# Order of the value products in the second mixer: upper and lower attention weights of a key block side by side

## The chip, the core and the metric

The kernel runs on one core of one Trainium2 chip. The metric is device time in microseconds, from the start of the program to its end. An execution with the profiler gives the trace from which every row below is taken; its own time and its span stand beside the median of the unprofiled runs.

## The reference: what is computed

A two-layer streaming encoder trunk for 1024 prompt frames and 8 x 16 sample frames (1152 columns in all), width 1024, in float32. Layer 0 has a first mixer (stick-breaking attention beside a convolution), layer 1 a second mixer (chunk-band attention with a learned relative bias); each layer ends with a squared-ReLU MLP of width 4096. The change is in the second mixer, whose attention is

```
s = einsum('bqhd,bkhd->bhqk', q, k) * HEAD_DIM**-0.5 + rel_bias[:, rel]
p = softmax(where(mask, s, -inf))          # own chunk of 64 and the 8 chunks before it
o = einsum('bhqk,bkhd->bqhd', p, v)
```

with 16 heads of 64. For the prompt a block of 128 queries sees at most five blocks of 128 keys.

## The kernel before

Activations lie transposed (features on partitions, tokens on columns). A float32 matrix product is made of float32r products: each operand is split into an upper part and a lower rest (`split`: ScalarE copies the upper part, L185, VectorE subtracts it for the rest, L186). A projection takes three products for one (upper-upper, upper-lower, lower-upper: `SPLIT`), so its first two follow each other on the same stationary weights.

The second mixer (`mixer1`) goes through 8 pairs of heads, p = 0 to 7. A pair has eight jobs, i = 0, 1 (the head) times t = 0 to 3 (256 queries). A job has two score steps (`one`: TensorE products of queries with upper keys, L1201, and lower keys, L1202, both on the same stationary queries; the softmax with maximum L1165 on VectorE, exponential L1168 on ScalarE, reciprocal L1169 and scaling L1170 on VectorE), and then its weighing steps, `split_weigh_steps`. These gather the key blocks of the job into groups of at most 512 columns: (256, 128) for t = 0, (256, 256) and (256, 128) for t = 1, (256, 256), (256, 256) and (128, 128) for t = 2 and 3; 144 groups in all. `turn` transposes a group's weights on TensorE (L455, tile `tp`, shown as tpc) and splits them into `wh` and `wl` (shown as whc and wlc). `prod` multiplies them with the values (L467, into the accumulator av, shown as avc): the stationary operand is a key block's values, upper and lower halves side by side, which occupy 128 columns; the moving operand is 256 or 128 columns of wh or wl. `finish` adds the two halves of av (L475 on ScalarE, L477 on VectorE) and stores the result in cat_d.

Between these steps stand the projections of the next pair (L225 into psc, 128x384), the sample streams' attention, and `expand` (L348 to L353: upper and lower keys and scaled queries of the next pair, each a 64x1024 operation on ScalarE or VectorE, with copies by DMA from GpSimd). For p = 7 there is no next pair; there `ready_chunks` loads finished pieces (cr) back from cat_d and splits them into cat, and `part_out` begins the output projection (L225 into psoa) on them.

The steps are merged into one program order by a table of costs (`merge`), and a scheduler of the language then sets each engine's final order from its own model of times: an instruction that its model holds back lets others on its engine pass. So a change of the order in one step can move instructions elsewhere. Each engine works through its own queue in order; ScalarE, VectorE, GpSimd and SyncE (which issues most loads) have one each.

Of the kernel before, what the change touches and what calls it, by code (L numbers as in the profile page):

```python
# [124 lines left out]
def tile_trunk(ctx, tc, ins, outs):  # L125
# [17 lines left out]
    def bank(name):  # L143
        return psum.tile([P, 512], F32, tag="ps", name=name)
# [38 lines left out]
    def split(hi, lo, src):  # L183

        ACT(hi, src, AF.Copy)  # L185
        return tt(lo, src, f(hi), ALU.subtract)  # L186
# [247 lines left out]
    def split_weigh_steps(vs, wk, cat, i, t, blocks, name, scored):  # L434


        order = sorted(blocks.keys, key=lambda j: -len(blocks.keys[j]))
        groups, cur, used = [], [], 0
        for j in order:
            n = P * len(blocks.keys[j])  # L440
            if used + n > 512:
                groups.append((cur, used))
                cur, used = [], 0
            cur.append((j, used, n))
            used += n
        groups.append((cur, used))
        nmm = 2 * len(order)
        st = {"done": 0, "w": {}}

        def turn(gi):  # L450
            items, used = groups[gi]
            tp = bank(f"tp{name}{gi}")
            for j, c0, n in items:
                for q, tile_q in enumerate(blocks.keys[j]):
                    nc.tensor.transpose(tp[:, c0 + q * P:c0 + (q + 1) * P], blocks.get(j, tile_q), ident)  # L455
            wh = wk.tile([P, 512], F32R, tag="wt", name=f"wh{name}{gi}")
            wl = wk.tile([P, 512], F32R, tag="wt", name=f"wl{name}{gi}")
            split(wh[:, :used], wl[:, :used], tp[:, :used])
            st["w"][gi] = (wh, wl)

        def prod(gi):
            if gi == 0:
                st["av"] = bank(f"av{name}")
            for src in st["w"][gi]:
                for j, c0, n in groups[gi][0]:
                    o0 = 0 if 2 * t in blocks.keys[j] else P
                    mm(st["av"][:, o0:o0 + n], vs[:, j, i].rearrange("p a d -> p (a d)"), src[:, c0:c0 + n],  # L467
                       start=st["done"] == 0, stop=st["done"] == nmm - 1)
                    st["done"] += 1

        def finish():
            own = slice(64 * i, 64 * i + 64)
            av = st["av"]
            tmp = wk.tile([P, 256], F32, tag="av", name=f"at{name}")
            ACT(tmp[own], av[64:128, :256], AF.Copy)  # L475
            piece = wk.tile([P, 256], F32, tag="cat", name=f"cp{name}")
            tt(piece[own], av[0:64, :256], tmp[own], ALU.add)  # L477
            cat.put(piece, own, t * 256, 256)

        def pcost(gi):  # L480
            return sum(2 * max(n, 256) * PASS for _, _, n in groups[gi][0])

        def tcost(gi):
            return groups[gi][1] / P * 109

        last = len(groups) - 1
        def dcost(gi):
            return 60 + groups[gi][1] / 0.96

        def turns(gi):  # L490
            return Step(tcost(gi), lambda: turn(gi), dcost(gi), f"turn{name}{gi}", None if gi else scored, 4500)

        lag = 4500 if cat.layer == 0 else 2500

        def prods(gi):
            if gi < last:
                return Step(pcost(gi), lambda: prod(gi), 0.0, None, f"turn{name}{gi}", lag)
            return Step(pcost(gi), lambda: (prod(gi), finish()), 330.0, f"out{name}", f"turn{name}{gi}", lag)

        steps = [turns(0)]  # L500
        for gi in range(1, last + 1):
            steps += [turns(gi), prods(gi - 1)]
        steps.append(prods(last))
        return steps
# [1441 lines left out]
```

## Time and profile before

| | us |
|---|---|
| median of 3 runs | 2752.49 (2751.73 to 2756.9) |
| the profiled execution, its own time | 2748.28 |
| its span, first to last instruction | 2746.5 |
| TensorE products (PE) busy | 2666.7, 97% |
| VectorE (DVE) / ScalarE (ACT) / GpSimd (POOL) busy | 2090.2 / 1388.1 / 328.2 |

The span is 1.8 us shorter than the execution's own time, which in turn is 4.2 us below the median of the unprofiled runs; differences worked out in the trace are added to the median. PE counts the products, PEld the loads of stationary weights that run beside them. In a row of a timeline the columns are start, duration, engine, line, operation, written tiles <- read tiles, shapes, and the count where equal instructions follow each other; in brackets the idle time of the engine before the first and what ended it. Ends of products are modelled, so consecutive products overlap in the rows: the distance between starts tells the pace.

### The profile page before, as it was taken

What the parts mean: (1) busy time and instruction counts of PE and PEld (TensorE: products, weight loads), DVE (VectorE), ACT (ScalarE), POOL (GpSimd) and SP (SyncE); (2) the same over time, 40 slices, a digit from 0 to 9 for tenths busy, and PEclk for the clock granted to TensorE, in tenths of its full rate; (3) what the DMA queues carried; (4) which work ended last, traced back from release to release, by engine and by line L of the source; (5) the groups of instructions that cost most, each with busy time, mean ns of one, the idle gap of its engine ahead of it and who ended that gap; (6) DMA issues with size and microseconds to landing.
All of it is one profiled execution on the core that took longest, in us unless ns stands there. A gap on an engine that the chain in (4) does not pass through costs nothing.

```text
span 2746.5 us, 50585 instructions
## 1 busy us (share of the span) xinstructions
PE 2666.7 (97%) x19362; PEld 2553.7 (93%) x19362; DVE 2090.2 (76%) x4117; ACT 1388.1 (51%) x2906; POOL 328.2 (12%) x599
## 2 busy tenths in 40 slices
PE   8999898999999999999999999998999999999998
PEld 8987776799999999999999999997999999999998
DVE  8999998888777755768577777778787777647577
ACT  5344457755444543435355555556555545434344
POOL 1000101041111100000011111110221111100001
PEclk9999999999999999999999999999999999999999
DMA  4434446454344377435444444446534334674344
GB/s 158 124 113 141 122 137 228 144 176 140 142 143 145 133 271 248 118 102 174 141 138 144 133 139 139 132 134 231 180 127 144 143 140 144 232 259 134 96 125 145
DMA packets 173203, 422.90 MB, mean 154 GB/s; under 512 B 25968, under 2 KB 53808, under 8 KB 170912
## 3 DMA queue, kind: packets, MB, share of 16 engines
q1 hardware_dynamic: 135696, 288.38, 33.4%
q0 software_dynamic: 37120, 131.27, 13.9%
q8 instruction: 152, 2.49, 0.4%
q14 instruction: 91, 0.75, 0.1%
q10 hardware_dynamic: 144, 0.02, 0.0%
HBM read 289.60 MB, written 117.34 MB: 148 GB/s over the span
## 4 chain that ended last, share of the span: by engine, by line
PE 71%; DVE 4%; ACT 2%; DMA 1%; issue 1%; DVEq 0%; SPq 0%; ACTq 0%; POOLq 0%
PE pd L1690 26%; PE um L1461 25%; PE psc L225 10%; PE avc L467 2%; PE tpc L455 2%; PE zc L1201 1%; PE zc L1202 1%; PE psoa L225 1%; PE so L602 1%; PE zs L568 1%; DVE xr L1367 0%; PE psob L225 0%; DMA cr<-cat_d 0%; ACT s L1168 0%; ACT whc L185 0%
## 5 line engine op out<-in xcount | busy, mean ns | idle before, releaser
L225 PE MATMUL psc<-h,hl_wc 128*128 128x384 f32 x1728 | 327.2, 340 | 0.0
L225 PEld LDWEIGHTS psc<-h,hl_wc 128*128 128x128 f32 x1728 | 296.9, 188 | 13.3 <-issue 10.9
L1461 PE MATMUL um<-sl,hl_m 128*128 128x288 f32 x1548 | 240.8, 296 | 0.0
L1461 PEld LDWEIGHTS um<-sl,hl_m 128*128 128x128 f32 x1548 | 218.2, 189 | 0.0
L1690 PE MATMUL pd<-tm,hl_wd 128*128 128x288 f32 x1584 | 214.7, 295 | 0.0
L1690 PEld LDWEIGHTS pd<-tm,hl_wd 128*128 128x128 f32 x1584 | 211.3, 189 | 0.0
L735 DVE SCALAR_TENSOR_TENSOR y<-u,dw,y 128x1024 f32<-128x1024 f32 (+1 forms) x232 | 178.1, 810 | 0.6
L225 PE MATMUL psp<-h,hl_wi 128*128 128x384 f32 x864 | 165.7, 344 | 0.0
L1468 ACT ACTIVATE hdm<-hdm 128x288 f32<-128x288 f32 x192 | 84.7, 442 | 156.5 <-DVE hdm L1467 154.8
L225 PEld LDWEIGHTS psp<-h,hl_wi 128*128 128x128 f32 x864 | 150.8, 191 | 6.8 <-issue 6.0
L186 DVE TENSOR_TENSOR tm<-xr,tm 128x576 fp32r<-128x576 f32 (+1 forms) x120 | 86.1, 718 | 92.4 <-ACT tm L185 92.3
L185 ACT ACTIVATE tm<-xr 128x576 fp32r<-128x576 f32 (+1 forms) x120 | 77.6, 647 | 94.7 <-PE pd L1690 76.2
L1168 ACT ACTIVATE s<-s,mxc 128x640 f32<-128x640 f32 (+4 forms) x128 | 88.8, 694 | 60.2 <-DVE mxc L1165 58.5
L1461 PE MATMUL um<-sl,hl 128*128 128x288 f32 x756 | 119.1, 296 | 0.0
L1690 PE MATMUL pd<-th,hl_wd 128*128 128x288 f32 x792 | 113.9, 297 | 4.0 <-DVE th L186 3.9
L1690 PEld LDWEIGHTS pd<-th,hl_wd 128*128 128x128 f32 x792 | 108.4, 190 | 4.9 <-DVE th L186 4.3
L1690 PE MATMUL pd<-xr,hl_wd 128*128 128x288 f32 x792 | 112.3, 296 | 0.0
L1690 PEld LDWEIGHTS pd<-xr,hl_wd 128*128 128x128 f32 x792 | 107.8, 190 | 0.0
L1461 PEld LDWEIGHTS um<-sl,hl 128*128 128x128 f32 x756 | 106.4, 188 | 0.8
L1690 PE MATMUL pd<-tm,hl 128*128 128x288 f32 x768 | 104.9, 295 | 0.0
L1690 PEld LDWEIGHTS pd<-tm,hl 128*128 128x128 f32 x768 | 103.1, 188 | 0.0
L185 ACT ACTIVATE whc<-tpc 128x512 fp32r<-128x512 f32 (+1 forms) x144 | 72.3, 522 | 46.6 <-PE tpc L455 44.8
(526 smaller groups left out, 6632.1 us busy)
## 6 DMA issues: line engine op xcount, KB each, us to landing
xr<-hb_d SPq DMA_DIRECT2D x208, 288.0 KB, 3.0
xr<-in_w_up_dram SPq DMA_DIRECT2D x64, 512.0 KB, 4.3
hb_d<-hdm POOLq DMA_DIRECT2D x96, 288.0 KB, 2.4
hb_d<-t POOLq DMA_DIRECT2D x96, 288.0 KB, 2.4
wm<-in_w_down_dram SPq DMA_DIRECT2D x64, 256.0 KB, 4.0
st_wd<-in_w_down_dram SPq DMA_DIRECT2D x64, 256.0 KB, 3.7
st_wc<-in_w_in_c_dram SPq DMA_DIRECT2D x44, 256.0 KB, 3.0
xm_d<-xo POOLq DMA_DIRECT2D x16, 576.0 KB, 3.5
```

The source lines that it names most:

```text
L185: ACT(hi, src, AF.Copy)
L186: return tt(lo, src, f(hi), ALU.subtract)
L225: mm(ps()[:, :G], hl[:, a, at:at + P], act[g][k // 4][b][:, k % 4, :], start=n == 0, stop=n == len(todo) - 1)
L455: nc.tensor.transpose(tp[:, c0 + q * P:c0 + (q + 1) * P], blocks.get(j, tile_q), ident)
L467: mm(st["av"][:, o0:o0 + n], vs[:, j, i].rearrange("p a d -> p (a d)"), src[:, c0:c0 + n], start=st["done"] == 0, stop=st["done"] == nmm - 1)
L568: mm(box["z"][at // 512][own, at % 512:at % 512 + kw], qb[:, own], k[:, b * kw:b * kw + kw], start=True, stop=True)
L602: mm(box["o"][own, 0:P], wt[k4][:, c:c + 32], v[:, at:at + P], start=False, stop=k4 == nz - 1 and j == 3)
L735: stt(src if j == CW - 1 else dst, src, wj, dst, ALU.mult, ALU.add)
L1168: ACT(s[:, :n], s[:, :n], AF.Exp, bias=mx, scale=-1.0, accum_out=tot)
L1461: mm(banks[b, n][:, :TQ], w[:, a, c * P:c * P + P], combo(key, c)[:, h, n * TQ:n * TQ + TQ], start=k < 3 and c == 0 and i == 0, stop=c == ...
L1468: ACT(y, y, AF.Relu)
L1690: mm(ps, w[:, a, m * P:m * P + P], b[:, h, (n - ns[0]) * TQ:(n - ns[0]) * TQ + TQ], start=first and s == 0, stop=j == NJ - 1 and s == 2, s ...
```

## The change

In `prod`, the two loops change places. Before, all key blocks of a group are multiplied with the upper weights and then all with the lower; after, each key block is multiplied with its upper and then its lower weights. The same products are summed into the same accumulator.

```
-            for src in st["w"][gi]:
-                for j, c0, n in groups[gi][0]:
+            for j, c0, n in groups[gi][0]:
+                for src in st["w"][gi]:
                     o0 = 0 if 2 * t in blocks.keys[j] else P
                     mm(st["av"][:, o0:o0 + n], vs[:, j, i].rearrange("p a d -> p (a d)"), src[:, c0:c0 + n],
                        start=st["done"] == 0, stop=st["done"] == nmm - 1)
```

What it makes of the engines' orders, at three places. TensorE in a job with t = 1 (two groups of two key blocks; whc and wlc are upper and lower weights, 128x256 and 128x128 the products' shapes):

```order
-L467 MATMUL avc_14763<-whc_14717,vs_14196 128x256 x2
-L467 MATMUL avc_14763<-wlc_14718,vs_14196 128x256 x2
+L467 MATMUL avc_14763<-whc_14717,vs_14196 128x256
+L467 MATMUL avc_14763<-wlc_14718,vs_14196 128x256
+L467 MATMUL avc_14763<-whc_14717,vs_14196 128x256
+L467 MATMUL avc_14763<-wlc_14718,vs_14196 128x256
 L467 MATMUL avc_14763<-whc_14725,vs_14196 128x256
+L467 MATMUL avc_14763<-wlc_14726,vs_14196 128x256
 L467 MATMUL avc_14763<-whc_14725,vs_14196 128x128
-L467 MATMUL avc_14763<-wlc_14726,vs_14196 128x256
```

The products stay together and only trade places; this is all that moves at most of the 144 groups.

VectorE at the turn from one pair to the next (in the jobs i = 1, t = 2 and 3 of a pair; l and q are the lower keys and the lower scaled queries of the next pair, L351 and L353; hl_wc is a weight tile of a later projection). Before:

```order
L1165 ISA s_16225,mxc_16232<-zc_16226,bp_15729 128x384
L1165 ISA mxc_16232 128x1
L186 TENSOR_TENSOR hl_wc_1_16293<-st_wc_1_16291,hl_wc_1_16293 128x512
L1165 ISA s_16225,mxc_16234<-zc_16229,bp_15729,mxc_16232 128x256
L1165 ISA mxc_16234 128x1
L186 TENSOR_TENSOR wlc_16244<-tpc_16240,whc_16243 128x256
L351 TENSOR_TENSOR l_14195<-sk_15759,k_14193 64x1024
L1169 RECIPROCAL totc_16236<-totc_16236 128x1
L477 TENSOR_TENSOR cpc_16257<-avc_16220,atc_16255 64x256
L1170 TENSOR_SCALAR s_16225<-s_16225,totc_16236 128x640
L353 SCALAR_TENSOR_TENSOR q_14191<-sq_15461,q_14191 64x1024
```

and now:

```order
L1165 ISA s_16225,mxc_16232<-zc_16226,bp_15729 128x384
L1165 ISA mxc_16232 128x1
L351 TENSOR_TENSOR l_14195<-sk_15759,k_14193 64x1024
L1165 ISA s_16225,mxc_16234<-zc_16229,bp_15729,mxc_16232 128x256
L1165 ISA mxc_16234 128x1
L186 TENSOR_TENSOR wlc_16244<-tpc_16240,whc_16243 128x256
L353 SCALAR_TENSOR_TENSOR q_14191<-sq_15461,q_14191 64x1024
L1169 RECIPROCAL totc_16236<-totc_16236 128x1
L186 TENSOR_TENSOR hl_wc_1_16293<-st_wc_1_16291,hl_wc_1_16293 128x512
L1170 TENSOR_SCALAR s_16225<-s_16225,totc_16236 128x640
L477 TENSOR_TENSOR cpc_16257<-avc_16220,atc_16255 64x256
```

Both conversions of the next pair have moved up, the second of them ahead of the scaling L1170 of the pair's last scores. The same happens at five turns, those from pair 1 to pair 6. On TensorE four projection products, which stood behind the transposes of these last scores, now stand ahead of them:

```order
 L225 MATMUL psc_17212<-h_41_13713,hl_wc_1_16834 128x384
 L225 MATMUL psc_17212<-h_40_13712,hl_wc_1_16834 128x384
+L225 MATMUL psc_17212<-h_50_13750,hl_wc_1_16834 128x384
+L225 MATMUL psc_17212<-h_51_13751,hl_wc_1_16834 128x384
+L225 MATMUL psc_17212<-h_50_13750,hl_wc_1_16834 128x384
+L225 MATMUL psc_17212<-h_60_13787,hl_wc_1_16834 128x384
 L455 MATMUL tpc_17203<-ident,s_17130 128x128
 L455 MATMUL tpc_17203<-ident,s_17073 128x128
```

So the transposes' place in TensorE's queue is four products later. On SyncE's queue a load of a bias tile (L1182) moves ahead of one of a weight tile (L192), and on GpSimd's one store of a finished piece moves behind the two MEMSETs that wait for that bias tile, at the same five turns.

ScalarE at the turn from pair 6 to pair 7 (whc_20851 are the upper weights of the last group, of two key blocks, of pair 6; cat_00 the upper part of the first piece cr that is loaded back):

```order
 L185 ACTIVATE whc_20800<-tpc_20795 128x512
 L185 ACTIVATE whc_20819<-tpc_20814 128x512
+L185 ACTIVATE cat_00_20806<-cr_20804 128x384 x3
 L185 ACTIVATE whc_20851<-tpc_20848 128x256
-L185 ACTIVATE cat_00_20806<-cr_20804 128x384 x3
+L1168 ACTIVATE s_20868,totc_20874<-s_20868,mxc_20872 128x128
```

and on TensorE at the same turn (vt are transposes of the values of pair 7):

```order
-L467 MATMUL avc_20843<-wlc_20820,vs_14196 128x256 x2
-L467 MATMUL avc_20843<-whc_20851,vs_14196 128x128 x2
-L467 MATMUL avc_20843<-wlc_20852,vs_14196 128x128 x2
-L1150 MATMUL vt_20878<-ident,sv_20514 128x128 x2
 L1150 MATMUL vt_20884<-ident,sv_20514 128x128 x3
-L1150 MATMUL vt_20890<-ident,sv_20514 128x128 x3
+L1150 MATMUL vt_20890<-ident,sv_20514 128x128
+L467 MATMUL avc_20843<-whc_20851,vs_14196 128x128
+L1150 MATMUL vt_20890<-ident,sv_20514 128x128 x2
```

The upper weights of the last group now stand behind the three copies of the piece that is loaded back, and the first product that needs them stands behind seven of the nine transposes of the values instead of one.

## Rows read from the trace of the kernel before

**Rows 1.** The page: busy time, share of the span and instructions of each engine; then TensorE's granted clock in 40 equal slices of the span, in tenths of full speed.

```profile
PE 2666.7 (97%) x19362; PEld 2553.7 (93%) x19362; DVE 2090.2 (76%) x4117; ACT 1388.1 (51%) x2906; POOL 328.2 (12%) x599
PEclk9999999999999999999999999999999999999999
```

**Rows 2.** Windows over the second mixer's eight pairs, 1376 to 1946 us, in five equal parts of which the first and the last are shown with the sum. Columns: window, length, busy time and instructions of PE, PEld, DVE, ACT, POOL, granted clock as a share of full speed, share of the DMA engines, GB/s.

```profile
1376.00:1490.00 114.00, 113.31 (x827) 107.14 (x826) 81.41 (x230) 60.21 (x141) 13.06 (x31) 1.00 0.45 140
...
1832.00:1946.00 114.00, 105.79 (x742) 97.89 (x742) 91.81 (x259) 65.00 (x159) 11.13 (x22) 0.97 0.58 191
sum 570.00, PE 553.25 PEld 519.30 DVE 426.58 ACT 311.10 POOL 67.27; mean PE 110.65 PEld 103.86 DVE 85.32 ACT 62.22 POOL 13.45
```

**Rows 3.** Waits in the same stretch: engine, line and tile that waited, what for; us in total, times, longest.

```profile
PEld avc L467 <- ACT whc L185: 11.0, 13, 1.4
...
PE avc L467 <- ACT whc L185: 7.3, 8, 1.1
...
PE tpc L455 <- DVE s L1170: 6.0, 8, 3.2
```

**Rows 4.** The value products, line 467: count, duration of one in ns (least, median, most; ends are modelled), first and last start, and shapes, counted once for each of the 144 groups by its first product.

```profile
L467 PE MATMUL avc<-whc,vs x288: 221/282/583, 1384.0 to 1941.7; 128*128 128x256 f32 x112, 128*128 128x128 f32 x32
L467 PE MATMUL avc<-wlc,vs x288: 220/280/562, 1384.2 to 1941.9; 128*128 128x256 f32 x112, 128*128 128x128 f32 x32
```

**Rows 5.** TensorE's timeline at a job of pair 1, without a wait, and at a group of two 128-column blocks further on.

```profile
1498.97 0.40 PE L467 MATMUL avc<-whc,vs 128*128 128x256 f32 x2
1499.21 0.40 PE L467 MATMUL avc<-wlc,vs 128*128 128x256 f32 x2
1499.45 0.34 PE L467 MATMUL avc<-whc,vs 128*128 128x256 f32 x2
...
1500.26 0.28 PE L1201 MATMUL zc<-k,q 128*128 128x256 f32 x1
1500.38 0.28 PE L1202 MATMUL zc<-l,q 128*128 128x256 f32 x1
1500.49 2.24 PE L225 MATMUL psc<-h,hl_wc 128*128 128x384 f32 x12
1502.58 0.60 PE L455 MATMUL tpc<-ident,s 128*128 128x128 f32 x4
...
1517.62 0.34 PE L467 MATMUL avc<-whc,vs 128*128 128x128 f32 x2
1517.80 0.39 PE L467 MATMUL avc<-wlc,vs 128*128 128x128 f32 x2
1518.02 0.28 PE L1201 MATMUL zc<-k,q 128*128 128x128 f32 x1
```

**Rows 6.** TensorE's timeline at the turn from pair 1 to pair 2.

```profile
1504.86 0.50 PE L467 MATMUL avc<-whc,vs 128*128 128x256 f32 x2 [1.14 <-ACT whc L185]
...
1507.39 0.44 PE L467 MATMUL avc<-whc,vs 128*128 128x128 f32 x2
...
1510.87 0.88 PE L455 MATMUL tpc<-ident,s 128*128 128x128 f32 x6 [0.39 <-DVE s L1170]
```

**Rows 7.** ScalarE's and VectorE's timelines at the same turn.

```profile
1505.87 1.06 ACT L348 ACTIVATE k<-sk 64x1024 fp32r<-64x1024 f32 x1 [0.57 <-PE zc L1201]
...
1506.08 0.55 DVE L1165 CUSTOM_DVE_ANT_0 s<-zc,bp 128x384 f32<-128x384 f32 x1
...
1506.56 0.69 DVE L186 TENSOR_TENSOR hl_wc<-st_wc,hl_wc 128x512 fp32r<-128x512 f32 x1
1507.16 0.48 DVE L1165 CUSTOM_DVE_ANT_0 s<-zc,bp,mxc 128x256 f32<-128x256 f32 x1
...
1507.56 0.42 DVE L186 TENSOR_TENSOR wlc<-tpc,whc 128x256 fp32r<-128x256 f32 x1
1508.01 1.22 DVE L351 TENSOR_TENSOR l<-sk,k 64x1024 fp32r<-64x1024 f32 x1
1509.40 0.16 DVE L1169 RECIPROCAL totc<-totc 128x1 f32<-128x1 f32 x1 [0.16 <-ACT s L1168]
1509.80 0.42 DVE L477 TENSOR_TENSOR cpc<-avc,atc 64x256 f32<-64x256 f32 x1 [0.24 <-ACT atc L475]
1510.26 0.55 DVE L1170 TENSOR_SCALAR s<-s,totc 128x640 f32<-128x640 f32 x1
1510.84 1.22 DVE L353 SCALAR_TENSOR_TENSOR q<-sq,q 64x1024 fp32r<-64x1024 f32 x1
```

**Rows 8.** The turn from pair 6 to pair 7: TensorE's and ScalarE's timelines, and one window over it (columns as in rows 2).

```profile
1861.97 0.91 PE L455 MATMUL tpc<-ident,s 128*128 128x128 f32 x6 [3.25 <-DVE s L1170]
...
1864.52 0.38 ACT L185 ACTIVATE whc<-tpc 128x256 fp32r<-128x256 f32 x1 [0.82 <-DVE wlc L186]
...
1866.21 0.52 PE L467 MATMUL avc<-whc,vs 128*128 128x128 f32 x2
...
1866.95 1.93 PE L1150 MATMUL vt<-ident,sv 128*128 128x128 f32 x8
1867.22 1.35 ACT L185 ACTIVATE cat<-cr 128x384 fp32r<-128x384 f32 x3 [2.31 <-DMA cr<-cat_d]
1868.53 0.56 PE L1201 MATMUL zc<-k,q 128*128 128x256 f32 x1
...
1863.00:1870.00 7.00, 6.74 (x32) 6.74 (x33) 3.88 (x10) 3.82 (x10) 0.19 (x1) 0.53 0.73 189
```

## The prediction, made before the changed kernel had run

> **What bounds the kernel now.** The page comes first: TensorE's products are busy for 2666.7 of the span's 2746.5 us, every other engine far less, and the clock stands at nine tenths or more in all 40 slices [rows 1]. So the time is the length of TensorE's queue plus its few waits. Next come the windows over the second mixer, 1376 to 1946 us, which alone holds line 467: 553.25 of 570 us are busy there, 113.31 of 114 in the first fifth and 105.79 in the last, the only fifth whose clock is below 1.00 [rows 2]. The reader is to see that at most 16.75 us of idling are to be had, half of them in the last fifth. The waits then say what the idling belongs to [rows 3]. Products of line 467 waited for upper weights (whc) 8 times, 7.3 us in all and 1.1 at most, and their weight loads 13 times. Transposes (tpc) waited 6.0 us for the last scaling of a softmax (s, L1170), 3.2 of it once. Last come the timelines at the places where the orders differ [rows 5 to 8].
>
> **The products themselves.** The change issues the same 576 products, 288 with each half of the weights [rows 4]. Two things can differ. The first is their pace. Where key blocks alternate, four products with 256 columns start 1498.97, 1499.21 (two on) and 1499.45 (four on), 0.12 us each, though each has other stationary values than the one before it. L1201 and L1202, with the same 256 columns, follow each other on one stationary operand and start at 1500.26, 1500.38, and the next product at 1500.49: 0.12 and 0.11 [rows 5]. A shared operand buys nothing there: every product has its own load (19362 of each [rows 1]), and it hides beside the product ahead. With 128 columns, line 467 needs (1518.02 − 1517.62) / 4 = 0.10 us each [rows 5]. By columns alone it would be less: 384 columns take (1502.58 − 1500.49) / 12 = 0.174, so 128 would take 0.058. Here a load does show, but it is still issued after the change. I take 0, ±0.5 us for rounding and edges.
>
> What if the chip did skip a load that repeats the one before? A group of 512 columns is two 256-blocks, one of 384 a 256 and a 128, and the last group for t = 2 and 3 two 128-blocks. So a head has 1 + 1 + 2 + 2 = 6 products of 128 columns with each half of the weights, and 16 heads 96. Each second product would save at most 0.10 − 0.058 = 0.042: 96 × 0.042 = 4.0 us. That is rival A.
>
> The Trainium skill bears on this in "TensorE: Matmul & The Clock Gate", Part 2, under "Step-by-step: what each phase is for": the load is a separate instruction so that one load can serve many matmuls, and the queue pulls loads ahead of running matmuls. By the first half the change sets up a saving that the sum would show as −4.0; by the second, with each product still bringing its load, it would show 0. The equal counts of loads and products are with the second.
>
> The second thing is when the operands are needed. A lower half used to come second or later by one or two products; now it comes directly behind the first upper one, so up to one product (0.12 us) of cover is lost in each group that is late. The loads waited for whc 13 times [rows 3]; taking that number for the groups that are late at all, 13 × 0.12 = 1.6 us is the most, and 0 the least, because in the other groups both halves were finished well ahead. VectorE's subtraction follows the copy, so it is the one that can be late. I take 0.1.
>
> **The five turns between pairs.** Here VectorE's order differs. At 1504.86 TensorE waits 1.14 us for whc [rows 6]; then it goes on with score products, which release L348 at 1505.87 [rows 7]. Those come some 0.1 us earlier in the new order, at most, since one product stands elsewhere. I follow VectorE from there with the old durations. The first L1165 is at 1506.08; L351, which needs L348's result (1505.76 + 1.06 = 1506.82), starts at about 1506.9 and lasts 1.22, to 1508.1. The second L1165 (0.48) ends at 1508.6, the lower weights (0.42) at 1509.0, L353 (1.22) at 1510.2, the reciprocal (0.16) at 1510.4, the weight split hl_wc (0.69) at 1511.0, and L1170 (0.55) at about 1511.5 [rows 7]. Before it ended at 1510.81. So the last scores of a pair are some 0.7 us later. Behind L1170 wait the transposes, which already waited 0.39 us [rows 6]. In the new order four projection products stand ahead of them, 4 × 0.174 = 0.70 us of work [rows 5], which was to be done after. That is the cover: 0.7 late, 0.7 of other work. If it were gone, each turn would lose 0.7.
>
> Other parts of the same turn: the group with two 128-blocks starts at 1507.39 [rows 6] and could start one projection product earlier, but its lower half, ready at 1509.0 instead of about 1508.0, is now the second product, so it may hold TensorE for up to 0.2. The loads that trade places on SyncE's queue, and GpSimd's store that now stands behind MEMSETs, feed work of much later groups, and I cost them at nothing; their cover is that distance. The net of a turn is −0.2 to +0.4, five turns −1 to +2. I take 0.
>
> **The turn from pair 6 to pair 7.** Before, whc of the last group is made at 1864.52 (0.38), and ScalarE then idles 2.31 us for the piece that a DMA brings back, and makes cat from 1867.22 in 1.35 [rows 8]. Now the three copies stand ahead, so whc is ready at 1867.22 + 1.35 + 0.38 = 1868.95, four us later. TensorE used to do the group's four products from 1866.21 to 1866.95 (0.74), then eight transposes to 1868.53 (1.58, 0.20 each) [rows 8]. Now it reaches the first product without those four and with two transposes still behind: 1868.53 − 0.74 − 0.40 = 1867.4. It idles 1868.95 − 1867.4 = 1.55 us.
>
> Part of this comes back. The window 1863 to 1870 shows a granted clock of 0.53 [rows 8], so nearly all of it is at 1.2 GHz, the lower of the two levels; 0.53 × 7 = 0.5 × 6.6 + 0.4, so it ends about 1869.6. It follows 3.25 us in which TensorE waited for L1170 [rows 8]. What is pushed behind that end runs at the full level in half the time: about 1.55 of half-clock time, a saving of 0.8. The turn costs 1.55 − 0.75 = 0.8, with bounds 0 (the copies' DMA lands early, or work of the queue fills the wait) and 1.6 (nothing comes back). The low clock itself is outside the change. Should it not come in another execution, 6.6 × 0.5 = 3.3 us are saved; as the wait ahead of it is the same, I take that it comes.
>
> **Sum.** 0 (−0.5 to 0.5) + 0.1 (0 to 1.6) + 0 (−1 to 2) + 0.8 (−2.5, without the low clock, to 1.6) = 0.9; bounds −4.0 and +5.7. The profiled execution's 2748.28 would become 2749.2. It lies 4.2 us below the median of the runs, 2752.49, on which I put the difference: 2753.4.
>
> **Rivals.** *A, repeated loads are skipped.* For it speaks that the 128-column products are slower than their columns. Against it: equal counts, and the pace of L1201 to L1202 [rows 5]. It gives 0.9 − 4.0: 2749.4. To become faster than a measurement of this kernel can tell from no change (0.2%, 5.5 us) the 192 products of 256 columns would each have to gain (5.5 − 3.1) / 192 = 0.0125 us as well, against which 0.12 and 0.11 of L1201 and L1202 speak.
>
> *B, the slower side: the conversion L353 ahead of the last scaling.* Its place is VectorE at the five turns. L353 (1.22 us [rows 7]) now delays L1170 at the end of every pair. If the four projection products ahead of the transposes give no cover (since TensorE comes to them late itself, or what stands behind the transposes has no other work in between), a turn loses up to 1.22, five 6.1; with the 0.8 of the last turn it is 6.9: 2759.4. It decides from (5.5 − 0.8) / 5 = 0.94 us for each turn. Against it stand VectorE's idle 0.16 and 0.24 us in the old order and the cpc subtraction (0.42) that moved behind [rows 7], which take 0.8 of the 1.22 back.
>
> *C, another low clock.* The 1.55 us of idling in the last turn keep the lower level for longer. If it lasts as long again, the cost is 1.6 + 3.3 = 4.9: 2757.4, within what counts as the same; beyond 5.5 from (5.5 − 1.6) / 0.5 = 7.8 us more. Against it: the wait is half as long as the one before the first drop.
>
> *D, that the change does nothing it is meant for* is the forecast itself.
>
> **How the numbers follow.** The forecast has 0.80, A 0.07, B 0.07, C 0.06. The range takes the bounds of the sum, 2748.5 to 2758.2; A's and C's centres lie in it, so it leaves out B, half of A and half of C. Faster by over 0.2%, under 2747.0: half of A and a little of the forecast's lower end, 0.05. Slower, over 2758.0: B, half of C: 0.10. The same: 0.85.
>
> **What would show it.** Line 467 again has 288 and 288 loads, at 0.12 and 0.10 us from start to start; 0.06 for every second one of 128 columns would be A. The products of line 467 wait for whc 5 to 9 us in total in the mixer, 7.3 before [rows 3], with one new wait of about 1.5 us at some 1867 us for whc behind cat. At the five turns L1170 ends about 0.7 us later while the wait of tpc stays near 0.4; 1.6 or more would be B. The clock in the windows after 1870 is 1.00 again; less would be C. I am wrong if the mixer's length, from the first to the last line 467, changes by more than 6 us, or if it stays and the time changes elsewhere.

## The result, and the profile after

The median went from 2752.49 us to 2761.61 (2760.31 to 2767.69, 5 runs): slower by 9.1 us, ratio 1.0037 with an interval of 1.0026 to 1.0048. The forecast was 2753.4, and the time lies outside its range, which ended at 2758.2. The profiled execution has a span of 2759.8 us, 13.3 more than the one before, of which 4.3 have nothing to do with the change: line 467 starts at 1388.3 instead of 1384.0, after a stretch in which both programs are the same and the low clock took 16.8 us instead of 11.7 (one minus the granted clock, summed over windows of 24 us). So the comparison goes by the stretch of line 467.

The page after, in the line that answers to [rows 1]:

```profile
PE 2678.2 (97%) x19362; PEld 2560.0 (93%) x19362; DVE 2090.2 (76%) x4117; ACT 1388.7 (50%) x2906; POOL 328.3 (12%) x599
```

The value products after (count, durations in ns, first and last start), which answer to [rows 4]:

```profile
L467 PE MATMUL avc<-whc,vs x288: 220/282/581, 1388.3 to 1956.5; 128*128 128x256 f32 x112, 128*128 128x128 f32 x32
L467 PE MATMUL avc<-wlc,vs x288: 221/280/562, 1388.4 to 1956.7; 128*128 128x256 f32 x112, 128*128 128x128 f32 x32
```

And the waits over the mixer after, 1380 to 1961, which answer to [rows 3]:

```profile
PEld avc L467 <- ACT whc L185: 13.3, 15, 1.9
PEld avc L467 <- DVE wlc L186: 9.1, 15, 1.9
PE avc L467 <- ACT whc L185: 8.9, 9, 1.6
...
PE tpc L455 <- DVE s L1170: 5.0, 7, 3.1
...
PE avc L467 <- DVE wlc L186: 2.2, 3, 1.7
```

Loads and products are as many as before and last as long. The stretch of line 467 is 1956.7 − 1388.3 = 568.4 us instead of 557.9: 10.5 more. But the waits show little of it: for TensorE's products whc costs 1.6 more than before and wlc 0.8 more, and the wait of the transposes is 1.0 shorter. What grew is the **busy** time of TensorE, with the same instructions: by 11.5 us over the span, of which 3.2 lie ahead of line 467, with the low clock there, 8.9 in the stretch itself (550.05 instead of 541.12), and behind it there is 0.6 less. A loss that stands in no row of waits has to be looked for by place. Setting the n-th product of line 467 of one trace beside the n-th of the other, the distance is constant for tens of products and then jumps: by 1.4 us at each of the five turns, between the 133rd product and the 145th and again every 72 products, 6.9 in all up to the 481st (471.3 us from the first before, 478.2 after), and by another 3.5 in the rest, the turn to pair 7 and pair 7 itself (86.6 us before, 90.1 after).

Here is the place on TensorE's timeline before, some 2.3 us behind [rows 6]; zs (L568) is the score of the sample streams, four products with 32 stationary columns each, which the trace shows as two instructions each:

```profile
1513.17 0.40 PE L467 MATMUL avc<-whc,vs 128*128 128x256 f32 x2
1513.41 0.41 PE L467 MATMUL avc<-wlc,vs 128*128 128x256 f32 x2
1513.65 0.39 PE L455 MATMUL tpc<-ident,s 128*128 128x128 f32 x2
1513.79 0.48 PE L467 MATMUL avc<-whc,vs 128*128 128x256 f32 x2
1514.11 0.40 PE L467 MATMUL avc<-wlc,vs 128*128 128x256 f32 x2
1514.44 1.06 PE L568 MATMUL zs<-ct12k,qb 128*32 128x512 f32 x8
1515.43 2.35 PE L225 MATMUL psc<-h,hl_wc 128*128 128x384 f32 x12
```

and after:

```profile
1517.37 0.28 PE L467 MATMUL avc<-whc,vs 128*128 128x256 f32 x1
1517.48 0.27 PE L455 MATMUL tpc<-ident,s 128*128 128x128 f32 x1
1517.78 0.39 PE L467 MATMUL avc<-wlc,vs 128*128 128x256 f32 x1
...
1518.27 0.36 PE L467 MATMUL avc<-whc,vs 128*128 128x256 f32 x1
1518.57 1.04 PE L568 MATMUL zs<-ct12k,qb 128*32 128x512 f32 x2
1519.54 0.39 PE L467 MATMUL avc<-wlc,vs 128*128 128x256 f32 x1
1519.76 0.28 PE L467 MATMUL avc<-whc,vs 128*128 128x256 f32 x1
1519.88 0.28 PE L467 MATMUL avc<-wlc,vs 128*128 128x256 f32 x1
1520.09 1.06 PE L568 MATMUL zs<-ct12k,qb 128*32 128x512 f32 x6
1521.08 2.35 PE L225 MATMUL psc<-h,hl_wc 128*128 128x384 f32 x12
```

Before, the four narrow products stand together and take 1515.43 − 1514.44 = 0.99 us. After, the scheduler has put the first of them ahead of three products of line 467. Alone it takes 1519.54 − 1518.57 = 0.97; the other three, together, again 0.99. In the order of TensorE's instructions the row of four has become one and three:

```order
-L467 MATMUL avc_16341<-whc_16325,vs_14196 128x256 x2
-L467 MATMUL avc_16341<-wlc_16326,vs_14196 128x256 x2
-L568 MATMUL zs_16357<-ct12k_16358,qb_14188 32x512 x4
+L467 MATMUL avc_16341<-whc_16325,vs_14196 128x256
+L568 MATMUL zs_16357<-ct12k_16358,qb_14188 32x512
+L467 MATMUL avc_16341<-wlc_16326,vs_14196 128x256
+L467 MATMUL avc_16341<-whc_16325,vs_14196 128x256
+L467 MATMUL avc_16341<-wlc_16326,vs_14196 128x256
+L568 MATMUL zs_16357<-ct12k_16358,qb_14188 32x512 x3
```

TensorE counts as busy all the time, so the profile shows no wait. From the first product of line 467 in these rows to the projection behind zs it is 1515.43 − 1513.17 = 2.26 before and 1521.08 − 1517.37 = 3.71 after.

The Trainium skill, "TensorE: Matmul & The Clock Gate", Part 3, "The mechanism", says that products at different tile positions of the array run concurrently, each starting some 4 ns behind the one before. The trace agrees that they run side by side, but the distance is larger: in the kernel before, the first four of the eight instructions start at 1514.438, .444, .451 and .458, some 7 ns apart.

The turn from pair 6 to pair 7 after, TensorE's wait and ScalarE's rows, which answer to [rows 8]:

```profile
1880.63 0.33 PE L467 MATMUL avc<-whc,vs 128*128 128x128 f32 x1 [1.64 <-ACT whc L185]
```

```profile
1878.96 1.35 ACT L185 ACTIVATE cat<-cr 128x384 fp32r<-128x384 f32 x3 [3.64 <-DMA cr<-cat_d]
1880.21 0.36 ACT L185 ACTIVATE whc<-tpc 128x256 fp32r<-128x256 f32 x1
```

The wait is the one that was forecast, 1.64 us where 1.55 was worked out; that it comes so near is in part luck, as e3 and e4 below show. The clock there, in windows of 5 us (granted clock in the third column from the end), before and then after:

```profile
1860.00:1865.00 5.00, 2.64 (x14) 2.38 (x15) 4.12 (x7) 1.67 (x4) 1.34 (x4) 0.77 0.96 264
1865.00:1870.00 5.00, 5.00 (x26) 5.00 (x26) 2.59 (x8) 2.73 (x7) 0.00 (x0) 0.55 0.59 159
1870.00:1875.00 5.00, 4.91 (x29) 3.09 (x29) 4.70 (x16) 3.73 (x12) 0.53 (x1) 1.00 0.94 331
```

```profile
1871.00:1876.00 5.00, 2.81 (x12) 2.42 (x13) 4.20 (x7) 1.51 (x3) 1.34 (x4) 0.59 0.92 241
1876.00:1881.00 5.00, 3.36 (x19) 3.11 (x18) 1.83 (x7) 2.04 (x7) 0.00 (x0) 0.73 0.73 184
1881.00:1886.00 5.00, 5.00 (x26) 3.62 (x24) 4.20 (x16) 3.06 (x9) 0.53 (x1) 0.66 0.75 244
```

Before, the low clock costs (0.23 + 0.45) × 5 = 3.4 us of work at full speed (one minus the granted clock, times the length), after (0.41 + 0.27 + 0.34) × 5 = 5.1: a second stretch of it follows.

### The profile page after: what moved, and what is told of

Read it like the earlier page. It is cut to its first block, busy times and chain, and to the rows that moved or that the text cites. A ratio compares the mean times of both kernels' runs of the same rounds, so it can differ in the third digit from the quotient of the medians.

```text
span 2759.8 us, 50580 instructions
## 1 busy us (share of the span) xinstructions
PE 2678.2 (97%) x19362; PEld 2560.0 (93%) x19362; DVE 2090.2 (76%) x4117; ACT 1388.7 (50%) x2906; POOL 328.3 (12%) x599
## 4 chain that ended last, share of the span: by engine, by line
PE 71%; DVE 4%; ACT 2%; DMA 1%; issue 1%; DVEq 0%; ACTq 0%; SPq 0%
PE pd L1690 26%; PE um L1461 25%; PE psc L225 10%; PE avc L467 2%; PE tpc L455 2%; PE zc L1201 1%; PE psoa L225 1%; PE zc L1202 1%; PE zs L568 1%; PE so L602 1%; DVE xr L1367 0%; PE psob L225 0%; DMA cr<-cat_d 0%; ACT whc L185 0%; DMA xr<-in_w_up_dram 0%
```

## The experiments

The table holds what they measured: the time, its ratio to the kernel before, run again beside each (medians of 2752.0 to 2752.9), and from the profile of each the length from the first product of line 467 to the 481st (all five turns), and from there to the last (the turn to pair 7 and pair 7).

| kernel | median us | ratio (95%) | to the 481st | from there |
|---|---|---|---|---|
| before | 2752.49 | | 471.28 | 86.6 |
| the change | 2761.61 | 1.0037 (1.0026 to 1.0048) | 478.21 | 90.1 |
| e1, not around the turns | 2752.36 | 1.0004 (0.9995 to 1.0013) | 471.24 | 87.5 |
| e2, pairs 0 to 5 only | 2759.66 | 1.0025 (1.0015 to 1.0035) | 478.24 | 87.5 |
| e3, pairs 6 and 7 only | 2756.34 | 1.0012 (1.0004 to 1.0021) | 471.30 | 88.3 |
| e4, narrow products kept together | 2754.61 | 1.0012 (1.0003 to 1.0022) | 472.45 | 92.2 |
| e5, before, zn inside the four | 2771.23 | 1.0070 (1.0057 to 1.0083) | 487.47 | 89.3 |
| e6, before, zn behind the four | 2753.03 | 1.0007 (0.9998 to 1.0016) | 472.31 | 87.9 |
| e7, not in i = 1, t = 3 | 2755.33 | 1.0008 (0.9999 to 1.0018) | 472.34 | 87.3 |
| e8, before, L353 later at the turn to pair 7 | 2750.45 | 0.9995 (0.9986 to 1.0004) | 471.25 | 86.9 |
| e9, before, weight copies later | 2751.26 | 0.9993 (0.9984 to 1.0002) | 471.30 | 86.3 |
| e10, pairs 0 to 5, narrow products together | 2752.36 | 0.9998 (0.9990 to 1.0007) | 472.43 | 87.7 |

The length to the 481st is the sharp measure: the clock is 1.00 in all of it, and kernels with the same order there agree within 0.07 us (before, e3, e8, e9, and e1, where only products of line 467 trade places; or the change and e2). The length behind it is not: with the order of before at the turn to pair 7 it lies between 86.3 and 87.9 (e5 left out, since two of its sixteen split steps lie there) and the low clock costs 1.7 to 5.1 us of full speed in it.

**e1, the order by itself.** The loop takes either order by a condition, here and in the next ones:

```
-            for src in st["w"][gi]:
-                for j, c0, n in groups[gi][0]:
+            w, items = st["w"][gi], groups[gi][0]
+            for src, (j, c0, n) in [(s, k) for k in items for s in w] if not (i == 1 and t >= 2) else [(s, k) for s in w for k in items]:
```

> Side by side everywhere except in the jobs i = 1, t = 2 and 3, that is at 96 of the 144 groups; VectorE, ScalarE, GpSimd and SyncE keep the order of the kernel before, only products of line 467 trade places. Stretch from the first to the last start of line 467: 557.9 us before, 568.4 after. Theory (the order itself costs nothing, the cost comes from what the scheduler moved around five turns and in the last pair): 557.9 within 0.5, time that of before. Rival (the order costs by itself, in pace or in lost cover): two thirds of the 10.5, so 564.9, and some 7 us on the time.

471.24 against 471.28: with two thirds of the groups in the new order, nothing is lost or won, neither by a shared stationary operand nor by lost cover. The whole stretch is 558.7, 0.9 longer, all of it behind the 481st product, where a second stretch of low clock came in this execution (5.1 us of full speed instead of 3.4).

**e2 and e3, where the time goes.** The conditions are `cat.p < 6` and `cat.p >= 6`.

> Side by side for pairs 0 to 5 only; the five turns then have the order of the changed kernel (one of four narrow score products of the samples, L568, ahead of three products of line 467, the other three behind), the turn from pair 6 to pair 7 that of before. Theory (each of these turns costs 1.4 and nothing else does before pair 6): stretch of line 467 557.9 + 7.0 = 564.9, time +7. Rival (the lost time is made mainly in the last pair and the turns are noise of one execution): 558 to 559, time within 1.5 of before.

> Side by side for pairs 6 and 7 only; the five turns as before, the turn from pair 6 to pair 7 and what follows as in the changed kernel. Theory (the two causes add): stretch of line 467 557.9 + 3.5 = 561.4, time +3.5, with a wait of about 1.6 us for the upper weights behind the copies of cat and a granted clock below 0.75 in a five-microsecond window more than before. Rival (the second low clock comes only of what the earlier turns did): about +1, 559.

The five turns cost 478.24 − 471.28 = 6.96, 1.39 each, in time 0.0025 × 2752 = 6.9 us. The last pair costs 0.0012 × 2752 = 3.3 us (1.1 to 5.8). Together 10.2, as much as the ratio of the whole change gives. The stretch of e3 is only 1.7 longer than before, between the 3.5 expected and the 1 of its rival, and its clock did not fall a second time (3.4 us of full speed, as before). So e3 shows that the last pair costs time by itself, but not where a second stretch of low clock comes from. TensorE's wait at the turn in its profile:

```profile
1876.11 0.33 PE L467 MATMUL avc<-whc,vs 128*128 128x128 f32 x1 [0.88 <-ACT whc L185]
```

**e4, the narrow products kept together.** The change with the four L568 pinned at five turns (pairs 2 to 6, first half of the samples):

```
-                mm(box["z"][at // 512][own, ...], qb[:, own], k[:, b * kw:b * kw + kw],
-                   start=True, stop=True)
+                pin = tc.keep_in_program_order if layer == 1 and 2 <= p < 7 and bg == 0 else lambda x: x
+                pin(mm(box["z"][at // 512][own, ...], qb[:, own], k[:, b * kw:b * kw + kw],
+                                            start=True, stop=True))
```

Nothing else moves against the changed kernel, on any engine.

> The changed kernel with one thing undone: at the five turns the four narrow products L568 are pinned in their place in the program and stand together behind the last product of line 467; all else has the order of the changed kernel. Theory (a narrow product alone takes as long as four side by side): 5 x 0.97 to 1.2 us come back, stretch 568.4 - 5.5 = 562.9, time 5 below the changed kernel. Rival (the narrow product filled a wait of TensorE for lower weights that VectorE makes later now): the wait of about 1 us appears in its place at each turn, stretch 568 within 0.5, time that of the changed kernel.

TensorE's timeline of e4 at the same place (one more line in the kernel, so L569 is the L568 of the others; in e5 and e6 too, where zn is L570):

```profile
1518.47 0.36 PE L467 MATMUL avc<-whc,vs 128*128 128x256 f32 x1
1518.67 0.29 PE L467 MATMUL avc<-wlc,vs 128*128 128x256 f32 x1
1518.80 0.28 PE L467 MATMUL avc<-whc,vs 128*128 128x256 f32 x1
1518.92 0.28 PE L467 MATMUL avc<-wlc,vs 128*128 128x256 f32 x1
1519.13 1.07 PE L569 MATMUL zs<-ct12k,qb 128*32 128x512 f32 x8
1520.12 2.38 PE L225 MATMUL psc<-h,hl_wc 128*128 128x384 f32 x12
```

478.21 − 472.45 = 5.76 come back, 1.15 for each turn, and no wait takes the place: the lower weights are there at 1518.67, 0.2 behind the upper product. So the narrow product filled no wait of that size, and the rival falls. 1.17 us, 0.23 for each turn, stay. The median came down by 2761.61 − 2754.61 = 7.0 us. In the profiled execution the stretch of line 467 came down by 3.7 only, because there the wait for whc in the last pair was longer than in the change:

```profile
1875.46 0.47 PE L467 MATMUL avc<-whc,vs 128*128 128x128 f32 x1 [3.04 <-ACT whc L185]
```

That wait is 0.88, 1.64 and 3.04 us in e3, the change and e4, whose order there is the same. It ends behind the landing of a DMA: the copies of cat start 11.75, 12.43 and 12.83 us behind the 481st product. And it begins when TensorE gets there, 12.54, 12.46 and 11.46 us behind it: in e4 the clock was low for 3.4 us on the way, in the other two for 6.8.

**e5 and e6, the price of a split by itself.** Both are the kernel before with the full-width product zn (L573, the samples' scores with their new keys), which came later, moved up to the narrow products of every sample step of the mixer: inside, behind the first of the four, or behind all of them.

```
             for b in range(4):
                 own = slice(32 * b, 32 * b + 32)
-                mm(box["z"][...][own, ...], qb[:, own], k[:, b * kw:b * kw + kw], start=True, stop=True)
+                pn = tc.keep_in_program_order if layer == 1 and b else lambda x: x
+                pn(mm(box["z"][...][own, ...], qb[:, own], k[:, b * kw:b * kw + kw], start=True, stop=True))
+                if layer == 1 and b == 0: box["zn"] = bank(f"zn{name}"); pn = tc.keep_in_program_order(mm(box["zn"][:, 0:P], qb, s["kn"], start=True, stop=True))
...
```

(`b == 3` in e6; pn pins the last three narrow products and zn; zn's old place, in the part left out, is empty in this mixer. The two programs differ in nothing else, and up to the 481st product neither do the orders of their engines; in pair 7 the scheduler moved some more.)

> The kernel before, its value products untouched, with one full-width product zn (L573) moved: at all 16 steps of the samples' scores in this mixer it stands between the first and the other three of the four narrow products L568. To be read against the next kernel. Theory (a narrow product alone lasts as long as four together, 0.97): stretch of line 467 longer by about 14 x 1.0 = 14 (14 of the 16 steps lie inside it), time +15. Rival (what cost time at the turns was the lower weights, not the split): longer by at most 0.1 at each, under 1.6 in all.

> The control of the kernel before this one: zn stands directly behind all four narrow products at the same 16 steps, all else as there. Both theories: stretch of line 467 557.9 within 1, time that of before within 2.

e5, one step on TensorE:

```profile
1521.99 1.04 PE L569 MATMUL zs<-ct12k,qb 128*32 128x512 f32 x2
1522.97 0.49 PE L570 MATMUL zn<-kn,qb 128*128 128x128 f32 x2
1523.38 1.06 PE L569 MATMUL zs<-ct12k,qb 128*32 128x512 f32 x6
1524.37 2.37 PE L225 MATMUL psc<-h,hl_wc 128*128 128x384 f32 x12
```

and e6:

```profile
1516.77 1.06 PE L569 MATMUL zs<-ct12k,qb 128*32 128x512 f32 x8
1517.77 0.49 PE L570 MATMUL zn<-kn,qb 128*128 128x128 f32 x2
1518.01 2.33 PE L225 MATMUL psc<-h,hl_wc 128*128 128x384 f32 x12
```

One step takes 2.38 us in e5 and 1.24 in e6: 0.98 for the product alone, and 0.17 more between zn and the product behind it (0.41 instead of 0.24), which is now a narrow one. Thirteen such steps lie between the first product of line 467 and the 481st: 487.47 − 472.31 = 15.2, 1.17 each, the price that e4 got back at the turns (1.15). Over all sixteen it would be 18.7; the medians differ by 18.2. The expected 1.0 for each was the product alone, without the switch behind it. Moving zn, which both do, costs 1.0 of its own, within what the time can show.

**e7, what the 0.2 is.** Side by side everywhere except in the jobs i = 1, t = 3 (`not (i == 1 and t == 3)`): the narrow products stay together, while VectorE's order at the turns is that of the change.

> Side by side everywhere except in the jobs i = 1, t = 3. VectorE's order at the five turns is that of the changed kernel (L351 and L353 moved up), the four narrow products stand together, and ScalarE's order, the turn to pair 7 with it, is that of before. Theory (the moved conversions are covered; the 0.23 us for each turn that stayed when the narrow products were kept together belong to the job i = 1, t = 3, whose lower weights are asked for one product earlier): first start of line 467 to the product that begins the turn to pair 7 (the 481st) 471.28 before, here 470.8 to 471.4, time that of before. Rival (the moved conversions cost them): 472.4, time +1.

472.34: the rival was right. The moved conversions, with the load and the store that move with them, do cost 0.21 for each turn, though the order at the place is that of before. TensorE's timeline of e7, to be read against the first two rows of before above, and VectorE's lower weights:

```profile
1515.37 0.87 PE L455 MATMUL tpc<-ident,s 128*128 128x128 f32 x6 [0.20 <-DVE s L1170]
1516.00 1.14 PE L225 MATMUL psc<-h,hl_wc 128*128 128x384 f32 x5
1516.98 0.41 PE L467 MATMUL avc<-whc,vs 128*128 128x256 f32 x2
1517.39 0.51 PE L467 MATMUL avc<-wlc,vs 128*128 128x256 f32 x2
```

```profile
1516.65 1.29 DVE L186 TENSOR_TENSOR wlc<-tpc,whc 128x512 fp32r<-128x512 f32 x2 [0.88 <-ACT whc L185]
```

The projection products behind the transposes before:

```profile
1511.50 1.84 PE L225 MATMUL psc<-h,hl_wc 128*128 128x384 f32 x9
```

Two upper products take 0.24 before and 0.41 here: the first lower product waits for wlc. The rows suggest why, though no run takes it apart further: L1170 and the transposes are later, so are the weights; the four projection products that cover this ahead of the transposes are missing behind them, where nine projection products stood before and five stand now, so TensorE comes to line 467 before VectorE is done.

**e10, both undone.** Side by side for pairs 0 to 5, with the narrow products pinned as in e4.

> Side by side for pairs 0 to 5, with the four narrow products L568 kept together at the five turns: both things that the runs so far name as dear are undone, while the value products of six pairs are still side by side and VectorE's conversions still moved up. Theory (0.2 us for each of the five turns is all that is left): first start of line 467 to the 481st 472.4 against 471.28 before, time +1, not to be told from before. Rival (something more in the order costs): +3 or more.

472.43, and the time of before within 0.1%: nothing else in the order costs anything that shows.

**e8 and e9, attempts at a faster one.** Both leave the value products alone. e8 queues L353 of the second head behind the last scaling at the turn to pair 7 (`tc.issue_after(S["sc"].ins)` around it, where S["sc"] is L1170); e9 pins ScalarE's copies of the projection weights in the program's order (`pin(ACT(hi, src, AF.Copy))` for names that begin with wc).

> The kernel before, its value products untouched; in the turn to pair 7 alone VectorE's conversion L353 of the second head is queued behind the scaling L1170 of the last scores, for which TensorE waits 3.25 us; a weight split (0.56) takes its place ahead of it. L1170 ends 1.22 - 0.56 = 0.66 earlier. If the granted clock stays as it is: wait 2.6, time -0.7, not to be told from before. If the shorter wait keeps the clock up: another 3.4 less, time -4.

> An attempt to beat both: the kernel before with its value products untouched; ScalarE's copies of the projection weights (hl_wc, L185, 0.61 us each) are queued behind what stands ahead of them in the program, so that they no longer stand ahead of whc at the turns, where TensorE waits 1.14 us for whc. TensorE's order stays. If the copy is what makes whc late: 0.6 less wait at each of five to seven turns, stretch of line 467 557.9 - 3 to 4, time -3. If the projections then wait for their weights instead: stretch the same or longer, with a wait of psc for hl_wc in its place.

In e8 TensorE's wait for L1170 became 2.33 us instead of 3.25, the clock fell all the same (3.4 us of full speed), and what was won was given back within the pair, where the scheduler had moved other instructions too: TensorE now waits 2.1 us for wlc instead of 1.4, and 1.5 instead of 1.0 for the pieces that go through cat.

```profile
PE psoa L225 <- DVE cpc L477: 1.5, 1, 1.5
```

The length from the 481st product is 86.9 against 86.6. In e9 the copy still stands ahead of whc at the turn that was meant, and the wait is 1.14 us as before: the edit did not reach it. Neither is to be told from before, and no version here beats it.

## Why the prediction was wrong

- **The products themselves: 0.** Right. e1 puts it at −0.04 us over five turns, and rival A is dead: a lower product behind its upper one costs what it did.
- **Lost cover, 0.1 with at most 1.6.** Within its bounds: loads of line 467 waited 9.1 us for wlc (2.1 before), but the products themselves 2.2 instead of 1.4, as most of a load's wait lies beside the product ahead of it.
- **The five turns, 0 with bounds −1 and +2.** The step that failed; it was +6.9. What the prediction worked out there held. L1170 was 0.7 us later by the sum and is 0.63 later by the trace (it ends at 1515.71, 1511.44 on the old time, instead of 1510.81), and the wait of the transposes was 0.23. But the working ended at the transposes. The sentence on the other parts of the turn listed the last group, the loads and the stores, and left out that the order showed L568 x4 taken apart, on TensorE's own queue. It costs 5 × 1.15 = 5.8. The other 1.1 is the cover of four projection products, which was counted as whole: it was taken from the place behind the transposes, where 0.2 us for each turn was needed.
- **The turn to pair 7, 0.8.** Mis-sized. The wait came out at 1.64 for 1.55 worked out; the term should have been about 3: e3 gives 3.3 us (1.1 to 5.8), and the three profiles with the new order have 88.3, 90.1 and 92.2 from the 481st product on, the eight with the old 86.3 to 87.9. The wait hangs on the landing of a DMA and on the clock ahead of it, so it is 0.88 to 3.04, where one execution had been taken for all; and in the profile of the change the clock did not give the 0.75 back but cost 5.1 − 3.4 = 1.7 more. How much of the 3 is this second stretch of low clock, rival C, stays open: it came with the waits of 1.64 and 3.04 us and not with the one of 0.88, but kernels with the old order (e1, e5, e6, e7) show a second stretch too, later in the pair.
- **Rival B** named the right turns and a time near the measured one, 2759.4, by a mechanism that did not occur: the wait of the transposes became shorter, not longer.
- **What would show it** asked for waits. The stretch of line 467, given there as the sign of being wrong, did show it; the waits could not, because TensorE was busy in the lost time.

## What to carry to other kernels

When an edit goes through a scheduler, read the whole difference of the slowest engine's queue for changes in what stands together, not only for what stands late: groups of narrow products that run side by side are one unit, and a full-width product between them cost as much here as the whole group and a little more (1.15 to 1.17 us for each group of 0.99). Such a loss has no idle time; compare the start of the n-th instruction of one line in both traces, and look where the distance jumps. Where work is moved ahead of a late operand as cover, ask what it covered at its old place.

## What was not expected of the hardware

- Four products with 32 stationary columns and 512 moving ones take 0.99 us together, three of them 0.99, one alone 0.97 to 0.98, here always in two instructions each.
- A full-width product between the first and the other three costs 1.15 to 1.17 us: 0.98 for the narrow product alone, and the other 0.17 to 0.19 where the rows of e5 show it, between the full-width product and the narrow ones behind it. All of it counts as busy.
